# The first half of the mixer projection: two f32r terms and three products against three bf16 terms and six products

## The chip, the cores and the metric

The kernel runs on one core of a Trainium2 chip. The metric is device time in microseconds (us), from one execution of the whole program. The core has five engines that run side by side: TensorE (PE in the profile, with its weight loads listed apart as PEld), VectorE (DVE), ScalarE (ACT), GpSimd (POOL) and SyncE (SP), which here only issues DMA transfers.

## What is computed

The reference is one step of a hybrid decoder layer: a Mamba-2 part and an mLSTM part read the same projected input, their outputs are put side by side and projected back, then come cross attention to a memory and a SwiGLU block, each with norms before and after. It works on 512 prompt tokens and 8 x 8 sample tokens, 576 in all, with a model width of 1024. What matters here is one line, the mixer projection:

```
y_ssd = _rms(y_ssd.reshape(..., SSM_GROUPS, SSM_INNER // SSM_GROUPS)).reshape(...) * g_ssm_out
...
mix = jnp.concatenate([y_ssd.astype(x.dtype), h_ml.astype(x.dtype)], axis=-1) @ w_out
x = x + _rms(mix) * g_post_mix
```

All of it is float32. w_out is 2048 x 1024: its upper 1024 rows meet y_ssd, the first half, and its lower 1024 rows meet h_ml, the second half.

## The kernel before, in words

Every activation lies transposed, features on the 128 partitions, in tiles of 128 x 8 x 576 (eight k-tiles of 128 features, 576 tokens). TensorE computes one output tile of 128 features at a time; the tokens are cut into two parts of 256 and 320 columns (HALVES).

To get nearly float32 precision, both operands are split into a high term, rounded to the type float32r, and the remainder as a low term. Three products are summed in PSUM: high x high, high x low of the activation, low of the weight x high. `split_w` (line 173) does this for weights: it loads 128 x 1024 floats into a buffer "raw" (two of them) through SP's queue, casts them on ACT into whi (line 181), and subtracts on DVE into wlo (line 188); whi and wlo have three buffers each. `split` (191) does the same for activations (ACT at 192, DVE at 193). `gemm` (195) issues the three products of each k-tile (201 to 203), each a matmul with its own weight load; `gemm2` (206) takes one PSUM bank for each half of the tokens and calls an evacuation when that half is done.

The stage that the change touches runs from line 1007 to line 1138. Ahead of it stand the last tiles of the input projection (the output gate of the mLSTM, `in_tile` with `og_evac`), and between them `gn_apply` (1014) scales each k-tile of y (the tile xs of slot 5) by its gain and norm and splits it into mixs_h and mixs_l. mixs_h lies in a pool "big0" on the right side of SBUF that takes over space of the sample mLSTM's pool, closed just ahead; mixs_l lies in slot 2. The splits of the second half's activations, mixm_h and mixm_l (1031, 1032, 1038), follow in the program.

The projection's first half is the loop at line 1133: for each of eight output tiles j, `split_w` of the weights I["wout"][j, 0], then `gemm2` for the first half of the tokens in a bank of pool GP and for the second half in a bank of pool MP (three banks each), each followed by a copy on ACT into f (tile f_mix, which has slot 5, that of y). `presplit` then does a piece of work for later: it loads a weight of the attention output or of the feed-forward part, splits it on ACT and DVE, and stores its low term to memory from GpSimd. The second half of the projection, `out2` (1166), runs the same products with mixm and I["wout"][j, 1], and adds f on DVE (line 1161).

Up to here the order on each engine is the scheduler's: it simulates the program in time and lets each engine take the instruction that is ready, so instructions of neighbouring loop turns mix. `issue_after` holds an instruction back until another has been issued. Later parts of the kernel are ordered by hand.

At the very start of the kernel, line 300 runs 24 bf16 matmuls of 128 x 256 on zeros, all with the same weights, to bring TensorE to its full clock. Line 612 holds bf16 matmuls of 512 columns with 80 rows, two for each of eight feature tiles in the Mamba-2 part.

Of the kernel before, what the change touches and what calls it, by code (L numbers as in the profile page):

```python
# [11 lines left out]
F32 = mybir.dt.float32  # L12
F32R = mybir.dt.float32r
BF16 = mybir.dt.bfloat16
AF = mybir.ActivationFunctionType
ALU = mybir.AluOpType
# [3 lines left out]
P = 128  # L20
T = 576
# [3 lines left out]
KT = 8  # L25
# [3 lines left out]
HALVES = [(0, 256), (256, 320)]  # L29
# [87 lines left out]
def build(nc, tc, ctx, I, O):  # L117
    V, A, G, S, TE = nc.vector, nc.scalar, nc.gpsimd, nc.sync, nc.tensor
    mm = TE.matmul

    cp = ctx.enter_context(tc.tile_pool(name="const", bufs=1))
    wp = ctx.enter_context(tc.tile_pool(name="weights", bufs=1))
# [8 lines left out]
    def SL(slot, name, dt=F32, shape=(P, KT, T)):  # L131

        return big.tile(list(shape), dt, name=name, tag="s%d" % slot, bufs=1)
# [8 lines left out]
    def BP(name="b"):  # L142
        return pb.tile([P, 512], F32, name=name, tag="b")
# [20 lines left out]
    def PAR(k, j=None, w=1):  # L164
        a, b = _cols[k]
        return par[:, a:b] if j is None else par[:, a + j:a + j + w]
# [4 lines left out]
    loads = []  # L171

    def split_w(src, n=1024, cut=CUT, acc=False, pool=None, to=None, raw=None):
        if raw is None:
            raw = wp.tile([P, 1024], F32, name="raw", tag="raw", bufs=2)
        loads.append(S.dma_start(raw[:, :n], src))
        if to:
            split(*to, raw[:, :n])
            return to
        hi, lo = [(pool or wp).tile([P, 1024], F32R, name=k, tag=k, bufs=NWX if pool else 3) for k in ("whi", "wlo")]  # L180
        A.copy(hi[:, :n], raw[:, :n])  # L181
        for e, a, b in ((V, 0, cut), (G, cut, n)):
            if b > a and e is G and acc:

                A.activation(lo[:, a:b], hi[:, a:b].bitcast(F32), AF.Copy, scale=-1.0)  # L185
                G.dma_start(lo[:, a:b], src[:, a:b], accum_op=ALU.add)  # L186
            elif b > a:
                e.tensor_tensor(lo[:, a:b], raw[:, a:b], hi[:, a:b].bitcast(F32), op=ALU.subtract)  # L188
        return hi, lo

    def split(hi, lo, src, eng=None):
        A.copy(hi, src)
        (eng or V).tensor_tensor(lo, src, hi.bitcast(F32), op=ALU.subtract)

    def gemm(ps, units, xh, xl, t0, n, k0=0, k1=None, order=None):

        tiles = [(hi[:, j * P:(j + 1) * P], lo[:, j * P:(j + 1) * P]) for hi, lo, nk in units for j in range(nk)]
        order = order or range(len(tiles))
        for i, k in list(enumerate(order))[k0:k1]:
            (wh, wl), ah, al = tiles[k], xh(k, t0, n), xl(k, t0, n)  # L200
            mm(ps, wh, ah, start=i == 0, stop=False)  # L201
            mm(ps, wh, al, start=False, stop=False)  # L202
            m = mm(ps, wl, ah, start=False, stop=i == len(tiles) - 1)  # L203
        return m

    def gemm2(units, xh, xl, evac, name, halves=(0, 1), alloc=None, order=None, parts=HALVES):
        for i in halves:
            t0, n = parts[i]
            ps = (alloc or GP)(name)[:, :n]
            m = gemm(ps, units, xh, xl, t0, n, order=order)  # L210
            evac(t0, n, ps)
        return m

    def act(t):
        return lambda k, t0, n: t[:, k, t0:t0 + n]


    pows, ssq_mm, rops, rows = [], [], [], []
# [124 lines left out]
    stop = gemm(ps0[2][1], [(*w2, KT)], U, UL, 256, 320, 0, NSS)  # L343
# [12 lines left out]
    stop = gemm(ps0[3][0], [(*w3, KT)], U, UL, 0, 256)  # L356
# [208 lines left out]
    y = xs  # L565
# [98 lines left out]
    for g in range(2):  # L664
        ps = BP("ps_xts")
# [5 lines left out]
    ps = BP("ps_bts")  # L671
# [7 lines left out]
    for g in range(2):  # L679
        for hb in range(2):  # L680
            dst = cpad[:, g, 4 * hb:4 * hb + 4, :].rearrange("p b t -> p (b t)")
            src = bc[:, 2 + g, TP + 32 * hb:TP + 32 * hb + 32]
# [4 lines left out]
    for g in range(2):  # L687
        psb = BP("ps_ls")
        pb3 = psb.rearrange("p (h t) -> p h t", h=8)
        for h in range(8):  # L690
            mm(psb[:, h * TS:(h + 1) * TS], sel[:80, 8 * g + h:8 * g + h + 1].to_broadcast([80, P]), cumst[:, TP:T],
               start=h == 0, stop=h == 7, skip_group_check=True)
# [8 lines left out]
        for h in range(8):  # L701
            k, j = h % 2, (8 * g + h) // 2
# [6 lines left out]
    ps = BP("ps_eg")  # L709
# [6 lines left out]
    for b in range(4):  # L716
# [3 lines left out]
        for g in range(2):  # L720
            for hb in (1, 0):
# [3 lines left out]
                   start=b == 0, stop=b == 3, skip_group_check=True)  # L725
        for hb in range(2):
# [4 lines left out]
            for g in range(2):  # L731
                ps = BP("ps_hu")
# [6 lines left out]
    ps = BP("ps_yt")  # L739
# [64 lines left out]
    def head_norm(num, ex, n4, pool, name):  # L804

        ss = pool.tile([P, n4], F32, name="hn_ss", tag="hn_ss", bufs=2)
        jk = pool.tile([P, 256], F32, name="hn_jk", tag="hn_jk", bufs=1)
        for c in range(n4):
            A.activation(jk, num[:, c, 0:256], AF.Square, accum_out=ss[:, c:c + 1])
        d = pool.tile([P, n4], F32, name="hn_d", tag="hn_d", bufs=2)  # L810
        den = num[:, :, 256:257].rearrange("p c o -> p (c o)")
        V.scalar_tensor_tensor(d, den, -1.0, den, op0=ALU.mult, op1=ALU.max)
        V.tensor_tensor(d, d, ex, op=ALU.max)
        V.reciprocal(d, d)
        v = pool.tile([P, n4], F32, name="hn_v", tag="hn_v", bufs=2)
        yy = pool.tile([P, n4], F32, name="hn_y", tag="hn_y", bufs=2)
        a = pool.tile([P, n4], F32, name="hn_a", tag="hn_a", bufs=2)
        V.tensor_tensor(v, d, d, op=ALU.mult)
        V.tensor_tensor(v, v, ss, op=ALU.mult)
        V.tensor_scalar(v, v, 1.0 / 256.0, EPS, op0=ALU.mult, op1=ALU.add)  # L820
        G.tensor_tensor(yy, v, C32("nhalf")[:, :n4], op=ALU.pow)
        V.tensor_tensor(a, yy, yy, op=ALU.mult)
        V.scalar_tensor_tensor(a, a, -0.5, v, op0=ALU.mult, op1=ALU.mult)
        V.scalar_tensor_tensor(a, a, 1.5, yy, op0=ALU.add, op1=ALU.mult)
        V.tensor_tensor(a, a, d, op=ALU.mult)
        return a

    for h in range(4):
        q, k = qk[:, h, :], qk[:, 4 + h, :]
# [16 lines left out]
        for c in range(4):  # L846
# [3 lines left out]
                        op=ALU.mult)  # L850
# [16 lines left out]
        f = head_norm(num, expnm[:, :, h:h + 1].rearrange("p c o -> p (c o)"), 4, mp_, "p")  # L867
# [89 lines left out]
    for hb in range(2):  # L957
# [6 lines left out]
        for b in range(4):  # L964
# [16 lines left out]
            for h in range(4):  # L981
                ps = BP("ps_cu")
# [13 lines left out]
        f = head_norm(num, ex, 1, ms, "s")  # L996
# [9 lines left out]

    big0 = ctx.enter_context(tc.tile_pool(name="big0", bufs=1, side="right", reuse_waits="tile"))

    def SL0(name, dt=F32R):
        return big0.tile([P, KT, T], dt, name=name, tag="s0", bufs=1)  # L1010

    mixs_h = SL0("mixs_h")
    mixs_l = SL(2, "mixs_l", F32R)
    def gn_apply(g):
        rb = gn_rc[g][0][:, 0:T]
        for j in range(4 * g, 4 * g + 4):
            V.scalar_tensor_tensor(y[:, j, :], y[:, j, :], PAR("g_ssm", j), rb, op0=ALU.mult, op1=ALU.mult)
            split(mixs_h[:, j, :], mixs_l[:, j, :], y[:, j, :])


    mixm_h = SL(3, "mixm_h", F32R)
# [77 lines left out]
    f = SL(5, "f_mix")  # L1099
# [8 lines left out]
    evs, ahead = [], []  # L1108

    def presplit(n):  # L1110

        while ahead:
            n_, c, t_ = ahead.pop(0)
            h_ = at.tile([P, 1024], F32R, name="preh", tag="prh", bufs=1)
            with tc.issue_after(evs[-1].ins):
                A.copy(h_[:, c], t_[:, c])
            V.tensor_tensor(t_[:, c], t_[:, c], h_[:, c].bitcast(F32), op=ALU.subtract)
            G.dma_start(pre[:, n_, c], t_[:, c])
        for _ in range(n):
            n_ = turns.pop(0)  # L1120
            k, j = PRE[n_]
            c = slice(512 if j == 5 else 0, 1024)
            t_ = at.tile([P, 1024], F32, name="prel", tag=("pr", "prl", "mv")[n_ % 3], bufs=1)
            G.dma_start(t_[:, c], I[{"xo": "wxo", "g": "wgate", "u": "wup"}[k]][j][:, c])
            ahead.append((n_, c, t_))
# [5 lines left out]
    rmem_b = at.tile([P, 256], F32, name="rmem_b")  # L1131
    ssqm, ssq = ssq_tile("ssqm"), ssq_tile("ssqo")
    for j in range(8):
        w = split_w(I["wout"][j, 0], cut=1024)
        for i, bank in enumerate((GP, MP)):
            gemm2([(*w, KT)], act(mixs_h), act(mixs_l), lambda t0, n, ps: evs.append(A.copy(f[:, j, t0:t0 + n], ps)),
                  "ps_o1", (i,), bank)
        presplit(1 if j else 2)

        if j > 3:  # L1140
            k2 = slice(2 * j - 8, 2 * j - 6)
            with tc.issue_after(loads[-1].ins):
                S.dma_start(memraw[:, k2, :], I["memT"][:, k2, :])
# [26 lines left out]
    x = SL(1, "x1")  # L1170
# [39 lines left out]
    m = out2(7, 0)  # L1210
    with tc.issue_after(m.ins):
        rc = rstd_cols([ssq], HCHUNKS[1], "po1", alloc=B0)
    m = out2(6, 0)
# [41 lines left out]


    qh = SL0("qh")
    ql = SL(2, "ql", F32R)
    qsm = at.tile([P, 8, TS], F32, name="qsm")
# [124 lines left out]
    mk, m = mem_key(3, wm[:2])  # L1384
    with tc.issue_after(m.ins):
        rc = rstd_cols([ssq], HCHUNKS[0], "po0", alloc=B0)
    mv, m = mem_value(3, wm[2:])
# [10 lines left out]
    m = xq(4, 1)  # L1398
    with tc.issue_after(m.ins):
        rc2[1] = rstd_cols([ssq2], HCHUNKS[1], "p21", alloc=B1)  # L1400
    m = xq(5, 1)
    with tc.issue_after(m.ins):
        rstd_rows(rc2[1][:, 2:3], CHUNKS[4:], rb2, B1)
    m = xq(6, 1)
# [34 lines left out]
    f = SL(4, "f_xo")  # L1439
# [202 lines left out]
    for n_, (key, p) in enumerate(order):  # L1642
        src = I[{"xo": "wxo", "g": "wgate", "u": "wup"}[key[0]]][key[1]]
# [46 lines left out]
    class Pair:  # L1690
# [72 lines left out]
        def bank(s):  # L1763
            return (MP if s.up else GP)("ps_u" if s.up else "ps_g")[:, :288]
# [568 lines left out]
    parts = [(c, d) for c in range(2) for d in range(2)]  # L2333
    xr, xt, ft = [], {}, {}
# [156 lines left out]
```

## Time and profile before

| | |
|---|---|
| median of 3 runs | 1104.03 us (1101.62 to 1104.86) |
| the profiled execution | 1104.28 us, span 1102.5 us |
| PE matmuls, weight loads | 8351 each |
| DMA | 182.34 MB, mean 165 GB/s |

The profiled execution is one run of the program whose instructions were recorded; its span is the time from the first to the last recorded instruction. Rows of a view give line, engine, operation, the tiles written and read (out<-in) and the shapes. "x128" is a count. In a tile's view, three numbers with slashes are the least, median and greatest duration in ns, followed by the first and last start in us. In a timeline, the first two numbers are start and length in us; a row with a count merges several instructions of one form, and its length reaches from the first start to the last end. In a row of the grouped lines, the numbers behind the bar are the total busy time in us, the mean ns of one, and the idle time before them. A matmul's duration includes the time until its results have drained, so consecutive matmuls overlap, and the distance between starts is a different number.

### The profile page before, as it was taken

Reading aid. Unit: us, or ns where it says so; the run is one execution under the profiler, and the core shown is the slowest. Engines: PE = TensorE matmul, PEld = TensorE weight load, DVE = VectorE, ACT = ScalarE, POOL = GpSimd, SP = SyncE. Lnnn points to the kernel's source line nnn. Section 1 sums busy time; section 2 is a strip of 40 time slices with the busy share of each in tenths; the row PEclk is TensorE's granted clock in tenths of the full one; section 3 lists DMA queues with packets and bytes.
Section 4 is the critical chain, followed back from the end, with each engine's and each line's share of the span. In section 5 each row is a group of like instructions: output and inputs, shape, how many; then the busy total and the mean of one; then the engine's idle time right before and its main releaser. Section 6 shows DMA issues by size and latency. Waiting matters only on the chain.

```text
span 1102.5 us, 21225 instructions
## 1 busy us (share of the span) xinstructions
PE 1089.3 (99%) x8351; PEld 1042.0 (95%) x8351; DVE 771.4 (70%) x1521; ACT 604.0 (55%) x1121; POOL 215.3 (20%) x301
## 2 busy tenths in 40 slices
PE   9999999999999999999999999999999999999997
PEld 8999889898998999999988889999999999999997
DVE  6797765558786784578755556676578879888655
ACT  6768523246563465566535445634565556555654
POOL 1333442323122121110144401100000210020000
PEclk9999999999999999999999999999999999999999
DMA  6776553425474438773477755652552863497432
GB/s 205 178 148 154 121 160 126 155 83 158 130 202 108 127 99 287 284 278 100 154 272 268 287 168 169 208 184 66 179 152 82 203 161 89 102 230 211 108 133 86
DMA packets 59432, 182.34 MB, mean 165 GB/s; under 512 B 6556, under 2 KB 10780, under 8 KB 58820
## 3 DMA queue, kind: packets, MB, share of 16 engines
q1 hardware_dynamic: 44324, 142.19, 38.4%
q0 software_dynamic: 14720, 38.28, 16.6%
q8 instruction: 65, 1.06, 0.4%
q10 hardware_dynamic: 288, 0.52, 0.1%
q14 instruction: 35, 0.29, 0.1%
HBM read 151.66 MB, written 29.30 MB: 164 GB/s over the span
## 4 chain that ended last, share of the span: by engine, by line
PE 82%; DVE 5%; DMA 4%; ACT 3%; issue 1%; POOL 0%; DVEq 0%; ACTq 0%; SPq 0%
PE ps_in L201 5%; PE ps_in L202 5%; PE ps_in L203 5%; PE ps_g L1770 3%; PE ps_g L1771 3%; PE ps_g L1772 3%; PE ps_u L1770 3%; PE ps_u L1771 3%; PE ps_u L1772 3%; PE ps_o L201 2%; PE ps_o L203 2%; PE ps_o L202 2%; PE ps_dn L201 2%; PE ps_dn L203 2%; PE ps_dn L202 2%; PE ps_dn L1978 2%
## 5 line engine op out<-in xcount | busy, mean ns | idle before, releaser
L203 PE MATMUL ps_in<-uh,wlo 128*128 128x256 f32 (+1 forms) x544 | 163.8, 301 | 0.7 <-DMA wlo<-win 0.4
L202 PE MATMUL ps_in<-ul,whi 128*128 128x256 f32 (+1 forms) x544 | 163.9, 301 | 0.0
L201 PE MATMUL ps_in<-uh,whi 128*128 128x256 f32 (+1 forms) x544 | 163.7, 301 | 0.0
L181 ACT CAST whi<-raw 128x1024 fp32r<-128x1024 f32 (+1 forms) x102 | 102.7, 1011 | 83.5 <-PE ps_in L202 28.7
L188 DVE TENSOR_TENSOR wlo<-raw,whi 128x512 fp32r<-128x512 f32 (+1 forms) x94 | 91.2, 972 | 50.6 <-ACT whi L181 48.8
L202 PEld LDWEIGHTS ps_in<-ul,whi 128*128 128x128 f32 x544 | 103.0, 189 | 2.9 <-issue 2.2
L203 PEld LDWEIGHTS ps_in<-uh,wlo 128*128 128x128 f32 x544 | 103.0, 190 | 2.4 <-DVE wlo L188 0.6
L201 PEld LDWEIGHTS ps_in<-uh,whi 128*128 128x128 f32 x544 | 103.0, 189 | 2.0 <-issue 0.8
L186 POOL DMA_DIRECT2D wlo<-win x32 | 28.0, 883 | 80.8 <-ACT wlo L185 64.2
L1770 PE MATMUL ps_g<-b,whi 128*128 128x288 f32 x144 | 42.5, 296 | 0.2 <-ACT cc L1829 0.2
L1771 PE MATMUL ps_u<-b,whi 128*128 128x288 f32 x144 | 42.5, 295 | 0.0
L1771 PE MATMUL ps_g<-b,whi 128*128 128x288 f32 x144 | 42.5, 295 | 0.0
L1770 PE MATMUL ps_u<-b,whi 128*128 128x288 f32 x144 | 42.5, 295 | 0.0
L201 PE MATMUL ps_xo<-qh,whi 128*128 128x288 f32 x128 | 38.3, 302 | 0.4 <-ACT whi L181 0.3
L203 PE MATMUL ps_o<-mixm_h,wlo 128*128 128x256 f32 (+1 forms) x128 | 38.1, 298 | 0.0
L201 PE MATMUL ps_o<-mixm_h,whi 128*128 128x256 f32 (+1 forms) x128 | 38.0, 297 | 0.0
L202 PE MATMUL ps_o<-mixm_l,whi 128*128 128x256 f32 (+1 forms) x128 | 37.9, 296 | 0.0
L203 PE MATMUL ps_xq<-u2h,wlo 128*128 128x320 f32 (+1 forms) x128 | 37.9, 296 | 0.0
L202 PE MATMUL ps_xq<-u2l,whi 128*128 128x320 f32 (+1 forms) x128 | 37.8, 297 | 0.0
L201 PE MATMUL ps_xq<-u2h,whi 128*128 128x320 f32 (+1 forms) x128 | 37.8, 300 | 0.0
L202 PE MATMUL ps_xo<-ql,whi 128*128 128x288 f32 x128 | 37.7, 295 | 0.0
L203 PE MATMUL ps_xo<-qh,wlo 128*128 128x288 f32 x128 | 37.5, 295 | 0.0
(785 smaller groups left out, 3895.3 us busy)
## 6 DMA issues: line engine op xcount, KB each, us to landing
raw<-win SPq DMA_DIRECT2D x35, 512.0 KB, 3.6
raw<-wout SPq DMA_DIRECT2D x17, 512.0 KB, 5.6
raw<-wxq SPq DMA_DIRECT2D x13, 512.0 KB, 3.7
raw<-wgate SPq DMA_DIRECT2D x13, 512.0 KB, 4.4
raw<-wup SPq DMA_DIRECT2D x13, 512.0 KB, 4.0
wlo<-win POOLq DMA_DIRECT2D x24, 256.0 KB, 5.6
kva<-kc SPq DMA_DIRECT2D x12, 512.0 KB, 6.5
kva<-vc SPq DMA_DIRECT2D x12, 512.0 KB, 6.6
```

The source lines that it names most:

```text
L181: A.copy(hi[:, :n], raw[:, :n])
L186: G.dma_start(lo[:, a:b], src[:, a:b], accum_op=ALU.add)
L188: e.tensor_tensor(lo[:, a:b], raw[:, a:b], hi[:, a:b].bitcast(F32), op=ALU.subtract)
L201: mm(ps, wh, ah, start=i == 0, stop=False)
L202: mm(ps, wh, al, start=False, stop=False)
L203: m = mm(ps, wl, ah, start=False, stop=i == len(tiles) - 1)
L1770: mm(ps, wh, b[0][:, k, :], start=start and k == 0, stop=False, skip_group_check=True)
L1771: mm(ps, wh, b[1][:, k, :], start=False, stop=False, skip_group_check=True)
L1772: m = mm(ps, wl, b[0][:, k, :], start=False, stop=k == 3, skip_group_check=True)
L1978: mm(ps, wh, bh, start=start and k == 0, stop=False, skip_group_check=True)
```

## The change

The first half of the projection gets three bf16 terms for each operand. `split3` makes them: a cast of x to bf16 (h), x minus h in place, a cast of the rest (m), and the rest minus m as the third term (l): two casts on ACT and two subtractions on DVE, in a chain, and x is overwritten. `split3_w` loads a weight tile as before and splits it; h and m share a buffer of the ring whi, l takes one of wlo. `gemm3` walks k, then the three weight terms, then the two halves of the tokens, then the activation terms: three with the first weight term, two with the second, one with the third. That makes six products per k-tile and half. Both banks are evacuated when the whole tile is done. mixs is now a tile of 16 x 576 bf16 for h and m in the place of mixs_h, and one for l in slot 2. The second half of the projection stays as it was.

```diff
+    def split3(dst, x):
+        h, m, l = dst
+        A.copy(h, x)
+        V.tensor_tensor(x, x, h, op=ALU.subtract)
+        A.copy(m, x)
+        V.tensor_tensor(l, x, m, op=ALU.subtract)
+
+    def split3_w(src):
+        raw = wp.tile([P, 1024], F32, name="raw", tag="raw", bufs=2)
+        loads.append(S.dma_start(raw, src))
+        a, b = [wp.tile([P, 2048], BF16, name=k, tag=k, bufs=3) for k in ("whi", "wlo")]
+        w = a[:, 0:1024], a[:, 1024:2048], b[:, 0:1024]
+        split3(w, raw)
+        return w
+
+    def gemm3(banks, w, x3, parts):
+        for k in range(KT):
+            for i, wt in enumerate(w):
+                for ps, (t0, n) in zip(banks, parts):
+                    for xt in x3[:3 - i]:
+                        mm(ps, wt[:, k * P:(k + 1) * P], xt[:, k, t0:t0 + n], start=k == 0 and i == 0 and xt is x3[0],
+                           stop=k == KT - 1 and i == 2)
...
-    mixs_h = SL0("mixs_h")
-    mixs_l = SL(2, "mixs_l", F32R)
+    mixs = SL0("mixs_hm", BF16, 2 * KT)
+    mixs = mixs[:, 0:KT, :], mixs[:, KT:2 * KT, :], SL(2, "mixs_l", BF16, (P, 2 * KT, T))[:, 0:KT, :]
...
-            split(mixs_h[:, j, :], mixs_l[:, j, :], y[:, j, :])
+            split3([t_[:, j, :] for t_ in mixs], y[:, j, :])
...
-        w = split_w(I["wout"][j, 0], cut=1024)
-        for i, bank in enumerate((GP, MP)):
-            gemm2([(*w, KT)], act(mixs_h), act(mixs_l), lambda t0, n, ps: evs.append(A.copy(f[:, j, t0:t0 + n], ps)),
-                  "ps_o1", (i,), bank)
+        w = split3_w(I["wout"][j, 0])
+        banks = [bank("ps_o1")[:, :n] for bank, (_, n) in zip((GP, MP), HALVES)]
+        gemm3(banks, w, mixs, HALVES)
+        for ps, p in zip(banks, HALVES):
+            evs.append(A.copy(f[:, j, p[0]:p[0] + p[1]], ps))
```

More of the change, by code (lines that the diff above doesn't have):

```diff
@@ L1007, in build, with SL0 @@
     big0 = ctx.enter_context(tc.tile_pool(name="big0", bufs=1, side="right", reuse_waits="tile"))
-    def SL0(name, dt=F32R):
-        return big0.tile([P, KT, T], dt, name=name, tag="s0", bufs=1)
-    mixs_h = SL0("mixs_h")
-    mixs_l = SL(2, "mixs_l", F32R)
+    def SL0(name, dt=F32R, kt=KT):
+        return big0.tile([P, kt, T], dt, name=name, tag="s0", bufs=1)
+    mixs = SL0("mixs_hm", BF16, 2 * KT)
+    mixs = mixs[:, 0:KT, :], mixs[:, KT:2 * KT, :], SL(2, "mixs_l", BF16, (P, 2 * KT, T))[:, 0:KT, :]
     def gn_apply(g):
```

## The prediction

> **What bounds the kernel now.** First the page, for which engine is never free:
>
> ```profile
> span 1102.5 us, 21225 instructions
> PE 1089.3 (99%) x8351; PEld 1042.0 (95%) x8351; DVE 771.4 (70%) x1521; ACT 604.0 (55%) x1121; POOL 215.3 (20%) x301
> PEclk9999999999999999999999999999999999999999
> ```
>
> TensorE (PE) is busy for 99% of the span at the full granted clock; VectorE (DVE) and ScalarE (ACT) have 30% and 45% free. So time is gained or lost by the matmul stream, unless a stage proves otherwise. The stage in question is eight output tiles with 48 matmuls each, 384 in all. The tile view of ps_o places it:
>
> ```profile
> L201 PE MATMUL ps_o<-mixs_h,whi x128: 279/298/317, 396.8 to 447.4; 128*128 128x256 f32 x64, 128*128 128x320 f32 x64
> L203 PE MATMUL ps_o<-mixs_h,wlo x128: 279/294/315, 397.6 to 447.7; 128*128 128x256 f32 x64, 128*128 128x320 f32 x64
> L201 PE MATMUL ps_o<-mixm_h,whi x128: 278/296/395, 447.9 to 502.1; 128*128 128x320 f32 x64, 128*128 128x256 f32 x64
> ```
>
> The windows are, from the start of the first mixs matmul to the start of the first mixm one, for the tile ps_o alone, and then for all work in this stage and in those around it:
>
> ```profile
> 396.82:447.87 51.05, 51.05 (x385) 50.99 (x385) 0.00 (x0) 5.75 (x15) 1.00 0.66 234
> 380.00:396.50 16.50, 16.50 (x123) 16.23 (x122) 11.09 (x40) 6.35 (x14) 3.33 (x4) 1.00 0.30 104
> 396.70:448.00 51.30, 51.30 (x387) 51.24 (x387) 33.23 (x44) 32.42 (x56) 8.98 (x15) 1.00 0.66 234
> 447.70:505.00 57.30, 56.08 (x424) 55.51 (x423) 38.79 (x70) 35.33 (x59) 8.16 (x15) 1.00 0.74 257
> ```
>
> The columns are window, length, then busy time and count of PE, weight loads (PEld), DVE, ACT, POOL (the first row has no POOL), granted clock, DMA share and GB/s. PE has no free time in this stage: 51.05 us for 384 matmuls is 132.9 ns each (x385 counts one that only begins at the edge). DVE is free for 18 us of it, ACT for 19. So the stage's length is the number of matmuls times the distance from one start to the next. That distance, not the duration in the rows, is the price, because matmuls overlap:
>
> ```profile
> 398.10 0.31 PE L201 MATMUL ps_o<-mixs_h,whi 128*128 128x320 f32 x1
> 398.24 0.28 PE L202 MATMUL ps_o<-mixs_l,whi 128*128 128x256 f32 x1
> 398.36 0.28 PE L203 MATMUL ps_o<-mixs_h,wlo 128*128 128x256 f32 x1
> 398.48 0.28 PE L201 MATMUL ps_o<-mixs_h,whi 128*128 128x256 f32 x1
> ```
>
> Starts are 140 ns apart after 320 columns and 120 ns after 256, while each matmul "lasts" about 300 ns. The distance follows the columns that stream through, and both have the same 128-column weights.
>
> **The matmuls.** The change takes away 8 tiles x 8 k x 2 halves x 3 products = 384 matmuls and puts in 8 x 8 x 2 x 6 = 768, of the same sizes (128x256 and 128x320, mean 288 columns), in bf16. Half the bytes help only if a bf16 column takes less time. The trace of before has few bf16 matmuls. The nearest are the 24 at the start, 128x256 with 128x128 weights, repeated on the same weights, a load for each; the last five of them ran at the full clock:
>
> ```profile
> 4.98 0.71 PE L300 MATMUL ps_warm<-wz 128*128 128x256 bf16 x5
> L300 PEld LDWEIGHTS <-wz x24: 98/152/152, 1.1 to 5.3; 128*128 128x128 bf16 x24
> L300 PE MATMUL ps_warm<-wz x24: 272/421/421, 1.1 to 5.4; 128*128 128x256 bf16 x24
> 248.00 0.61 PE L612 MATMUL ps_l<-cumst,c 80*128 80x512 bf16 x2
> L612 PE MATMUL ps_l<-cumst,c x16: 377/381/392, 134.0 to 248.2; 80*128 80x512 bf16 x16
> ```
>
> Five in 0.71 us, the last one lasting 0.272 (the minimum, at the full clock), start (0.71 - 0.272) / 4 = 109.5 ns apart: 0.428 ns per column, so 123.2 ns for 288. That is 7% below the 132.9 of now, nowhere near half. The other bf16 row is a pair in the middle of the kernel, 512 columns: 0.61 - 0.381 = 0.23 us apart, 0.447 ns per column, so 129 ns for 288. And if bf16 went no faster than f32r, 132.9 stays. The new stage is then:
>
> - by the first row 768 x 123.2 ns = 94.6 us, which is 43.6 more than 51.05;
> - by the pair 768 x 129 = 99.1 us, 48.0 more;
> - at today's distance 768 x 132.9 = 102.1 us, 51.0 more.
>
> I take the first: same rows, same weights, same columns, and five in a stream, where the pair stands alone with 80 rows. The other two stay as the upper end.
>
> "Both halves in a row" puts up to six matmuls on one weight term. A gain would need that a load is left out or that loads set the pace. Neither shows: the page has 8351 loads for 8351 matmuls, and the 24 of L300, which do repeat one weight tile, have 24 loads. So I put the order at nothing.
>
> A rule that would make it worth more is weighed here. The loads get shorter: 98 ns in the row above, against 188 for the f32 ones:
>
> ```profile
> L203 PEld LDWEIGHTS ps_o<-mixs_h,wlo 128*128 128x128 f32 x128 | 24.1, 189 | 0.0
> L202 PEld LDWEIGHTS ps_o<-mixs_l,whi 128*128 128x128 f32 x128 | 24.0, 188 | 0.1
> ```
>
> The Trainium skill ("TensorE: Matmul & The Clock Gate", section "Weight-path perf modes — Fast Weight Load (FWL) and DoubleRow") says that full 128-column weights that are not fp32 load faster, measured about 2x. The two rows agree with it (98 against 188). The same place says that it wins with few columns per matmul; were the loads the pace here, halving the distance to 66.5 ns would make 768 matmuls cost 51 us and the change nothing. What the distances say of that stands with the rivals.
>
> **The weight splits.** A split now is one cast and one subtraction of 128x1024; it becomes two of each, in a chain of four over the same raw tile, written over in place:
>
> ```profile
> L188 DVE TENSOR_TENSOR wlo<-raw,whi 128x1024 fp32r<-128x1024 f32 x8 | 9.8, 1219 | 0.9 <-ACT whi L181 0.9
> L181 ACT CAST whi<-raw 128x1024 fp32r<-128x1024 f32 x8 | 8.4, 1046 | 1.1 <-PE ps_o L202 1.1
> ```
>
> Eight tiles add 8 x 1.05 = 8.4 us to ACT and 8 x 1.22 = 9.8 to DVE. The chain of one tile becomes 2 x (1.05 + 1.22) = 4.5 us, and one tile of matmuls will last 94.6 / 8 = 11.8, so it is hidden; only the first two fall in the stage before, where DVE has 16.5 - 11.1 = 5.4 us free per 16.5 and ACT 10. If that cover failed, the first tile would come 1.05 + 1.22 = 2.3 us late. The raw tile is held that much longer, so the next weight load, queued on SP for that buffer, goes out 2.3 us later; there are two raw buffers and a tile every 11.8 us. The slots are the same three of 4 KB a partition (hi and mid share one). Priced at nothing.
>
> **The activation splits.** These are at the edge, because the first matmuls wait for them; the casts begin at 395.8, a microsecond ahead of PE:
>
> ```profile
> 395.82 4.69 ACT L192 CAST mixs_h<-xs 128x576 fp32r<-128x576 f32 x8
> 396.53 0.76 DVE L193 TENSOR_TENSOR mixs_l<-xs,mixs_h 128x576 fp32r<-128x576 f32 x1
> 397.61 4.76 DVE L193 TENSOR_TENSOR mixs_l<-xs,mixs_h 128x576 fp32r<-128x576 f32 x7
> 396.82 0.55 PE L201 MATMUL ps_o<-mixs_h,whi 128*128 128x256 f32 x3
> ```
>
> Eight casts take 4.69 us on ACT, seven subtractions 4.76 on DVE (0.68 each); both double. DVE then needs 16 x 0.68 = 10.9 us from 396.5, to about 407.9 with the 0.4 of other work it does between. PE consumes the eight k-tiles of its first output tile in 11.8 us, to 408.6. So production keeps just ahead if casts and subtractions of neighbouring k-tiles overlap, and I add 1 us for the start, where mid needs cast, subtraction and cast (0.67 + 0.76 + 0.67 = 2.1 us) before it exists, against the 12 x 0.123 = 1.5 us that PE has per k-tile. If each k-tile's chain of four ran alone, 2.9 us each, eight take 22.9 us and PE would wait about 11. Behind these, queued on DVE and ACT, are the splits of the other half's activations (mixm), first used a whole stage later, and the evacuation into f_mix, which takes the buffer of y and so waits for its last subtraction, about 408; a tile has three banks in each pool, so PE doesn't feel it.
>
> **The rest.** 16 evacuations stay; both of a tile now come at its end, and the next tile has other banks. The 1.2 us that PE is idle in the next stage (57.30 - 56.08) may shrink, since DVE, ACT and the DMA queues get 44 us more to run ahead; I count that only in the low end.
>
> **Sum.** +43.6 (matmuls) + 1.0 (start) = +44.6 us on the profiled execution of 1104.28 us (span 1102.5): 1148.9. The median of the runs shown, 1104.03, lies 0.25 below it: 1148.6.
>
> **Rivals.** *Same pace as f32r*: the 9 ns gained in L300 come from repeating one tile on an idle memory, and in the stage, with DMA at 0.66, bf16 takes 132.9. For it: the pair at L612 at 129. Then +51.0 + 1.0, so 1156.0.
>
> *The splits starve the first tile*: the chain of four runs k-tile by k-tile. Then 11 us of waiting instead of 1, about 1159. Against it: now ACT runs its eight casts without waiting for the subtractions.
>
> *No slower, because loads set the pace.* PEld is busy 50.99 of 51.05 us, as full as PE. If a matmul cannot start sooner because its weights take 188 ns, bf16's 98 ns brings the distance to 132.9 x 98 / 188 = 69.3 ns: 768 x 69.3 = 53.2 us, +2.2, and 1106.2. It decides at (51.05 + 3.3) / 768 = 71 ns; below that the change costs less than the 0.3%, 3.3 us, that a measurement of this kernel can tell from none. The Trainium skill ("Perfetto Trace Analysis", section "Identifying the Most-Contended Engine") indeed says to judge TensorE by matmul FLOPs and by the busy share of LDWEIGHTS rather than by matmul busy time; taken so, 95% would name the loads. Against it in the rows: with equal loads the distance goes with the columns (120 and 140 ns), and L300, with loads of 98 ns, still starts only every 109.5.
>
> *It doesn't do what it says*: the scheduler, which orders instructions itself, breaks up the rows of equal weights. By the above that costs nothing.
>
> **How the numbers follow.** Forecast 0.81, same pace 0.11, starving 0.05, loads 0.02 (no slower), 0.01 for a gain I don't see. Predicted 1148.6. The low end is the forecast without the start and with the 1.2 us regained, and 1% off the stage for the rounding of 0.71: 1148.6 - 1.0 - 1.2 - 1.0 = 1145.4, so 1145. The high end takes in the pair and the same pace, 1157. Slower by over 0.3%: 0.97; within: 0.02; faster: 0.01.
>
> **What would show it.** PE count 8735 (+384), PEld too. In the stage, starts 109 to 110 ns apart after 256 columns and about 137 after 320; first matmul still near 397, second half beginning near 492, everything behind it shifted by 44 to 45 us and otherwise alike. Sixteen casts and sixteen subtractions of 128x576 from 395.8 to about 408, with PE idle for around 1 us before its second tile. I am wrong if the stage's 768 matmuls start 71 ns apart or less, if fewer than 8735 loads appear and the stage is shorter than 94 us, or if PE's idle time in the first tile is over 3 us.

## The result and the profile after

The changed kernel takes 1163.24 us (median of 4 runs, 1162.78 to 1164.86) against 1102.82 us for the kernel before in the same comparison: a ratio of 1.0538, with a 95% interval of 1.0513 to 1.0564. That is about 60 us slower. The forecast was 44.6 us slower, and 1163 lies above the top of its range, 1157. The profiled execution took 1162.78 us, its span is 1161.0, 58.5 more than before.

The page of the changed kernel, the lines that answer to those shown of before:

```profile
span 1161.0 us, 22029 instructions
PE 1135.6 (98%) x8735; PEld 1067.3 (92%) x8735; DVE 786.5 (68%) x1537; ACT 616.3 (53%) x1137; POOL 216.8 (19%) x301
PEclk9999999999999889999999999999999999999999
```

PE has 384 more matmuls and as many more loads, as forecast: no load is left out. But its busy share is lower, and the clock row, all nines before, has two eights where the new stage begins. The window view of ps_o, from the first mixs matmul to the first mixm one (columns as before):

```profile
401.94:507.89 105.95, 97.21 (x769) 0.03 (x1) 0.00 (x0) 4.85 (x14) 0.93 0.43 142
```

(This view does not count the bf16 loads with the tile, hence the 0.03; over all tiles they take 76.22 us in this window.) The same view of all work, in the stretch at the low clock and behind the stage, reads:

```profile
399.90:417.00 17.10, 6.33 (x26) 3.63 (x26) 16.97 (x27) 15.16 (x27) 4.13 (x6) 0.50 0.34 124
507.89:1161.00 653.11, 644.60 (x4976) 626.81 (x4973) 454.85 (x853) 359.18 (x681) 89.76 (x95) 1.00 0.56 168
```

The stage has grown from 51.05 to 105.95 us, begins at 401.9 in place of 396.8, and PE works in 97.2 of it. For 17.1 us the granted clock is 0.50, and in that stretch PE is busy for 6.3 us while DVE and ACT are full (17.0 and 15.2). What follows the stage takes 653.11 us; in the kernel before, by the same view:

```profile
447.87:1102.50 654.63, 644.55 (x4975) 626.47 (x4973) 456.05 (x854) 359.53 (x681) 92.11 (x100) 1.00 0.56 172
```

So the 58.5 us lie in the stage and at its start. What PE waited for, by the view of waits:

```profile
PE ps_o L240 <- ACT mixs_hm L222: 6.4, 1, 6.4
PE ps_o L240 <- ACT mixs_hm L220: 4.3, 1, 4.3
PE ps_o L240 <- DVE mixs_l L223: 2.3, 1, 2.3
```

The columns are total, times, longest. Each wait is for one term of the activations: 4.3 us for the first high term (L220), 6.4 for the first mid term (L222), 2.3 for the first low one (L223), 13.0 in all. The timelines show why they come late. PE, with the wait before each first matmul in brackets:

```profile
397.23 0.38 PE L1027 MATMUL ps_hts<-c,hns 128*128 128x128 f32 x2
401.94 1.60 PE L240 MATMUL ps_o<-mixs_hm,whi 128*128 128x256 bf16 x6 [4.33 <-ACT mixs_hm L220]
409.97 1.60 PE L240 MATMUL ps_o<-mixs_hm,whi 128*128 128x256 bf16 x6 [6.43 <-ACT mixs_hm L222]
413.87 0.64 PE L240 MATMUL ps_o<-mixs_l,whi 128*128 128x256 bf16 x2 [2.30 <-DVE mixs_l L223]
```

ACT, which casts:

```profile
397.55 1.06 ACT L220 CAST whi<-raw 128x1024 bf16<-128x1024 f32 x1
398.50 2.56 ACT L1057 ACTIVATE mixm_h<-qk,ghalf 128x512 fp32r<-128x512 f32 x4
401.21 4.69 ACT L220 CAST mixs_hm<-xs 128x576 bf16<-128x576 f32 x8
406.48 1.94 ACT L1057 ACTIVATE mixm_h<-qk,ghalf 128x512 fp32r<-128x512 f32 x3
408.31 1.04 ACT L222 CAST whi<-raw 128x1024 bf16<-128x1024 f32 x1
409.25 4.68 ACT L222 CAST mixs_hm<-xs 128x576 bf16<-128x576 f32 x8
```

DVE, which subtracts:

```profile
399.78 2.73 DVE L1058 SCALAR_TENSOR_TENSOR mixm_l<-qk,ghalf,mixm_h 128x512 fp32r<-128x512 f32 x4
402.77 5.43 DVE L221 TENSOR_TENSOR xs<-xs,mixs_hm 128x576 f32<-128x576 f32 x8
413.07 5.43 DVE L223 TENSOR_TENSOR mixs_l<-xs,mixs_hm 128x576 bf16<-128x576 f32 x8
```

The scheduler did not let the chains of neighbouring k-tiles overlap. It put all eight high casts, then all eight subtractions, then all eight mid casts, then all eight low subtractions; and ahead of and between these phases it put work that is due later: the splits of the second half's activations (mixm, L1057 and L1058) and of the third output tile's weights (whi, at 397.55 and 408.31). So the first mid term exists at 409.9 and the first low one at 413.8, when PE had been free since 397.6. PE meanwhile does six products of high terms, one in each of its six banks (three output tiles, two halves), and stops.

The distances, on the other hand, are those of the sum. From the PE timeline later in the stage:

```profile
420.61 0.27 PE L240 MATMUL ps_o<-mixs_l,whi 128*128 128x256 bf16 x1
420.72 0.43 PE L240 MATMUL ps_o<-mixs_hm,whi 128*128 128x320 bf16 x2
420.99 0.30 PE L240 MATMUL ps_o<-mixs_l,whi 128*128 128x320 bf16 x1
421.13 0.65 PE L240 MATMUL ps_o<-mixs_hm,whi 128*128 128x256 bf16 x4
```

0.11 us after 256 columns and 0.14 after 320 (0.27 for two).

### The profile page after: what moved, and what is told of

Its sections match the earlier page's. It is cut to its first block, busy times and chain, and to the rows that moved or that the text cites. A ratio compares the mean times of both kernels' runs of the same rounds, so it can differ in the third digit from the quotient of the medians.

```text
span 1161.0 us, 22029 instructions
## 1 busy us (share of the span) xinstructions
PE 1135.6 (98%) x8735; PEld 1067.3 (92%) x8735; DVE 786.5 (68%) x1537; ACT 616.3 (53%) x1137; POOL 216.8 (19%) x301
## 4 chain that ended last, share of the span: by engine, by line
PE 84%; DVE 4%; DMA 4%; ACT 3%; issue 1%; POOL 1%; DVEq 0%; ACTq 0%; SPq 0%; POOLq 0%
PE ps_o L240 8%; PE ps_in L201 4%; PE ps_in L202 4%; PE ps_in L203 4%; PE ps_g L1797 3%; PE ps_g L1798 3%; PE ps_g L1799 3%; PE ps_u L1797 3%; PE ps_u L1798 3%; PE ps_u L1799 3%; PE ps_dn L201 2%; PE ps_dn L203 2%; PE ps_dn L202 2%; PE ps_dn L2005 2%; PE ps_dn L2006 2%; PE ps_v L808 2%
## 5 line engine op out<-in xcount | busy, mean ns | idle before, releaser
L181 ACT CAST whi<-raw 128x1024 fp32r<-128x1024 f32 (+1 forms) x94 | 94.4, 1008 | 111.7 <-PE ps_o L240 26.6
L188 DVE TENSOR_TENSOR wlo<-raw,whi 128x512 fp32r<-128x512 f32 (+1 forms) x86 | 81.3, 947 | 77.5 <-ACT whi L181 75.9
L240 PE MATMUL ps_o<-mixs_hm,whi 128*128 128x320 bf16 (+1 forms) x512 | 90.9, 292 | 10.8 <-ACT mixs_hm L222 6.4
L240 PEld LDWEIGHTS <-whi 128*128 128x128 bf16 x640 | 63.7, 99 | 29.2 <-issue 13.9
L240 PE MATMUL ps_o<-mixs_l,whi 128*128 128x256 bf16 (+1 forms) x128 | 36.3, 289 | 2.3 <-DVE mixs_l L223 2.3
```

What stands on the lines that cost most here:

```text
L240: mm(ps, wt[:, k * P:(k + 1) * P], xt[:, k, t0:t0 + n], start=k == 0 and i == 0 and xt is x3[0], stop=k == KT - 1 and i == 2)
```

## The experiments

The theory after the result: the 768 matmuls cost what was forecast, and the 16 us beyond it are the three waits and the halved clock around them. The rivals: the stage is long through the bf16 matmuls themselves, or the equal weights in a row matter after all. All ratios are against the kernel before, run on the same chip; the changed kernel's is 1.0538 (1.0513 to 1.0564).

**The chain first.** The chains of the k-tiles are interleaved by force, and everything that stood between is held behind them.

```diff
+            with tc.issue_after(chain[j - 2][0].ins) if j > 1 else ExitStack(), \
+                    tc.issue_after(chain[j - 2][1].ins) if j > 1 else ExitStack():
+                chain.append(split3([t_[:, j, :] for t_ in mixs], y[:, j, :]))   # returns the m cast and the l subtraction
...
+    with tc.issue_after(chain[7][0].ins), tc.issue_after(chain[7][1].ins):
         for j in range(8):      # the mixm splits; also split3_w for j > 1
```

> The changed kernel, with the activation splits forced into the order h0 h1 m0 h2 m1 ... on ScalarE and s0 s1 l0 s2 l1 ... on VectorE, and with the splits of the second half's activations and of the third and later weight tiles held behind them. Nothing is left out. Theory A (the 768 matmuls cost what was forecast, 94 us; the other 16 us are TensorE waiting 13.1 us for mid and low terms, and its halved clock after it): the first casts move from 401.2 to about 398, TensorE waits 2 to 4 us in the first tile in place of 13.1, the clock stays up or drops shortly, time 1148 to 1153 us. Rival B (the stage is long because of the bf16 matmuls themselves): no change, 1161 to 1165 us.

1150.14 us, ratio 1.0422 (1.0397 to 1.0446). Its waits for the terms:

```profile
PE ps_o L239 <- ACT mixs_hm L222: 1.2, 1, 1.2
PE ps_o L239 <- ACT mixs_hm L220: 1.1, 1, 1.1
PE ps_o L239 <- DVE mixs_l L222: 0.4, 1, 0.4
```

Its stage in the window view of ps_o:

```profile
397.69:495.05 97.36, 95.82 (x768) 0.03 (x1) 0.00 (x0) 4.92 (x14) 0.98 0.44 150
```

The waits fall from 13.0 to 2.7 us, the stage from 105.95 to 97.36, and the whole kernel by 13 us, with all 768 matmuls still there. The rival that the bf16 matmuls are slow is out; 1150.1 is 1.5 us above the forecast of 1148.6.

**The other work later, the phases left.** Only the second of the two edits.

> The changed kernel, with only the second half's activation splits and the third and later weight splits held behind the last mid cast and the last low subtraction; the four phases (eight h, eight subtractions, eight m, eight l) are left as the scheduler puts them. Nothing is left out. Theory A: the phases start at about 398 without other work between them, m0 follows h7 at about 402.5 and l0 at about 404, so TensorE waits 5 to 7 us, with some of the clock drop left: 1154 to 1158 us. Rival A2 (the phase order does the harm, not the other work ahead of it): still about 10 us of waiting, 1159 to 1164 us.

1154.97 us, ratio 1.0467 (1.0442 to 1.0492). The mid term is now late by its phase alone, as the timeline of ACT shows:

```profile
397.67 4.68 ACT L220 CAST mixs_hm<-xs 128x576 bf16<-128x576 f32 x8
402.94 4.67 ACT L222 CAST mixs_hm<-xs 128x576 bf16<-128x576 f32 x8
```

Its waits:

```profile
PE ps_o L239 <- ACT mixs_hm L222: 4.6, 1, 4.6
PE ps_o L239 <- ACT mixs_hm L220: 1.1, 1, 1.1
PE ps_o L239 <- DVE mixs_l L222: 0.4, 1, 0.4
```

Waits of 6.1 us, as expected.

**The interleaving alone.** Only the first of the two edits.

> The changed kernel with only the forced order h0 h1 m0 h2 m1 ... and s0 s1 l0 s2 ...; the second half's activation splits and the third weight tile stay where the scheduler puts them, between. Nothing is left out. If both things do harm on their own (phases 5 us, other work ahead 8 us, from the two runs before), this gives 1156 to 1161 us. If the interleaving alone suffices: 1148 to 1152 us. If it is worth nothing without the other: 1161 to 1165 us or above.

1157.13 us, ratio 1.0469 (1.0424 to 1.0513), waits of 4.3, 3.0 and 0.9 us. So each of the two edits saves about as much: 8 us and 6 us alone (0.7% by either ratio), and 13 us (1.2%) together.

**The high and mid terms earlier.** No order is forced; two tiles change places.

```diff
-    mixs = SL0("mixs_hm", BF16, 2 * KT)
-    mixs = mixs[:, 0:KT, :], mixs[:, KT:2 * KT, :], SL(2, "mixs_l", BF16, (P, 2 * KT, T))[:, 0:KT, :]
+    mixs = SL(2, "mixs_hm", BF16, (P, 2 * KT, T))
+    mixs = mixs[:, 0:KT, :], mixs[:, KT:2 * KT, :], SL0("mixs_l", BF16, 2 * KT)[:, 0:KT, :]
```

> The changed kernel with one placement changed: the tile of the high and mid terms lies in slot 2, which is free earlier, and the low terms in the place of mixs_h. Nothing is left out and no order is forced. Casts, first subtractions and mid casts can then run under the output gate's matmuls, and only the eight low subtractions (5.4 us) are left at the edge. Theory A (TensorE's waits are the chain left without cover): its waits at the edge fall from 13.1 to 0 to 2 us, the clock stays up, 1146 to 1150 us, as forecast before. Rival (work moved ahead delays the output gate's evacuations instead): 1152 us or above.

1149.87 us, ratio 1.0401 (1.0357 to 1.0445). The timeline of ACT:

```profile
380.59 4.69 ACT L220 CAST mixs_hm<-xs 128x576 bf16<-128x576 f32 x8 [1.92 <-PE ps_c L885]
```

and that of PE:

```profile
399.17 0.41 PE L240 MATMUL ps_o<-mixs_l,whi 128*128 128x256 bf16 x2 [2.60 <-DVE mixs_l L223]
```

The high casts run at 380.6, under the matmuls of the stage before, against 397.7 in the kernel that only moves the other work: their place comes free 17 us sooner. PE waits once, 2.6 us (a little over the 0 to 2 expected), for the low terms; the 1.1 us for the first high term, which remain with the chain first, are gone. The buffer, which the prediction took as given, was the lever.

**f32r with the chain of four.** The kernel before, with only the activation split made as long as the new one (the last subtraction's result is not used).

```diff
-            split(mixs_h[:, j, :], mixs_l[:, j, :], y[:, j, :])
+            A.copy(mixs_h[:, j, :], y[:, j, :])
+            V.tensor_tensor(y[:, j, :], y[:, j, :], mixs_h[:, j, :].bitcast(F32), op=ALU.subtract)
+            A.copy(mixs_l[:, j, :], y[:, j, :])
+            V.tensor_tensor(y[:, j, :], y[:, j, :], mixs_l[:, j, :].bitcast(F32), op=ALU.subtract)
```

> The kernel before, f32r and three products, with only the activation splits of the first half turned into the chain of four (cast, subtraction in place, cast of the rest into the low term, one more subtraction whose result nobody reads). Nothing is left out. Theory A (the chain, not bf16, makes TensorE wait): the low term of the first k-tile exists only behind all eight casts and the mixm casts that the scheduler puts between, near 405 in place of 397.3, so TensorE waits 4 to 8 us, and its clock drops: 1107 to 1114 us. Rival (the waiting belongs to the bf16 kernel's weights or order): 1101 to 1105 us.

1112.71 us, ratio 1.0076 (1.0047 to 1.0105). Its waits in the stage:

```profile
PE ps_o L201 <- ACT whi L181: 4.0, 1, 4.0
PE ps_o L202 <- ACT mixs_l L1020: 3.4, 1, 3.4
```

The stage in the window view of ps_o:

```profile
396.65:457.93 61.28, 53.89 (x385) 53.31 (x386) 0.00 (x0) 5.91 (x15) 0.92 0.65 224
```

The first wait is put down to the weights of the third output tile. PE comes to them so early because the first two tiles stand still without their low term: after four products of high terms it stops, where in the kernel before the first product with the low term follows at 397.35. Without any bf16, PE waits 7.4 us in the same place, and its 384 matmuls take 53.9 us in place of 51.05 at a mean clock of 0.92. The chain alone makes the stall.

**Two bf16 terms.** The third terms and their three products are left out in this and the next two kernels.

```diff
-        V.tensor_tensor(x, x, h, op=ALU.subtract)
-        A.copy(m, x)
-        V.tensor_tensor(l, x, m, op=ALU.subtract)
+        V.tensor_tensor(m, x, h, op=ALU.subtract)
...
-            for i, wt in enumerate(w):
+            for i, wt in enumerate(w[:2]):
...
-                    for xt in x3[:3 - i]:
+                    for xt in x3[:2 - i]:
```

> The changed kernel with two bf16 terms and three products (the third term of weights and activations and the three products with the smallest weight are left out, so that the result is less exact). Theory A, by the distance of 109 and 136 ns: 384 x 122.5 ns = 47.0 us for the stage in place of 51.05 before, so 1098 to 1100 us, with no starvation, since the chain is again one cast and one subtraction. Rival B (bf16 goes at 132.9 or slower in the stage): 1102 to 1104 us or above.

1107.2 us, ratio 1.0027 (1.0013 to 1.0042): the stage came out as expected, the time did not. The window view of ps_o:

```profile
396.39:443.35 46.96, 46.96 (x385) 0.03 (x1) 0.00 (x0) 4.80 (x14) 1.00 0.63 218
```

of all work, from there to the query projection's first matmul:

```profile
443.35:515.42 72.07, 67.27 (x502) 66.79 (x500) 49.19 (x92) 43.51 (x78) 8.70 (x16) 0.95 0.68 238
```

and the longest wait in that stretch:

```profile
PE ps_ss L250 <- DVE ssqm L291: 4.8, 1, 4.8
```

384 matmuls in 46.96 us are 122.3 ns each (123.2 forecast), 4.1 us less than in f32r. But the stretch behind it takes 72.07 us; in the kernel before it is 66.35:

```profile
447.87:514.22 66.35, 65.13 (x501) 64.56 (x500) 48.01 (x91) 42.20 (x76) 8.16 (x15) 1.00 0.67 233
```

PE reaches the memory norm's sums earlier, waits 4.8 us there (1.2 before) and loses clock behind that (0.95). The gain is given back, and more: from there to the end it takes 590.78 us in place of 588.28, with a wait of 2.4 us for the sums of a later norm (0.5 before).

**The memory norm later.** The same kernel, with one call moved.

```diff
-    memory_norm()
     for j in range(4, 8):
         out2(j, 1)
+    memory_norm()
```

> Two bf16 terms and three products (the third term and its products are left out, as in the run with two terms), and the memory norm's sums, for which TensorE waited 4.8 us there, moved behind the next four half tiles of the second half. Theory: the 4.1 us gained in the stage are no longer given back to that wait and the halved clock behind it: 1097 to 1101 us. Rival (the wait only moves on to another point, since ScalarE, VectorE and the transfers of the second half set its pace): 1104 to 1108 us.

1103.6 us, ratio 1.0000 (0.9981 to 1.0018). That wait is gone, but PE now waits elsewhere, by the view of waits:

```profile
PE ps_os L1370 <- DMA kva<-vc: 2.0, 2, 1.1
PE ps_o L203 <- DVE wlo L188: 1.6, 2, 0.9
PE ps_o L201 <- ACT whi L181: 1.1, 1, 1.1
```

2.7 us for weight splits in the second half and 2.0 for a transfer in the attention (0.4 before). The time lies between what the theory gave (at most 1101) and the rival (at least 1104), nearer to the rival: the 4.1 us are gone by the end, and these waits, behind the stage, are the ones that are new.

**Both halves in two terms.** The kernel just above, with the second half in bf16 too.

```diff
-    mixm_h = SL(3, "mixm_h", F32R)
-    mixm_l = SL(4, "mixm_l", F32R)
+    mixm_h = SL(3, "mixm_h", BF16, (P, 2 * KT, T))[:, 0:KT, :]
+    mixm_l = SL(4, "mixm_l", BF16, (P, 2 * KT, T))[:, 0:KT, :]
...
+            kept2[j] = split3_w(I["wout"][j, 1])[:2]
```

> As the run before it, with the second half of the projection in two bf16 terms and three products too (third terms left out in both halves). By the distances 384 x 10.4 ns = another 4 us off: 1093 to 1097 us. Rival (the second half is already paced by the splits and transfers around it): no better than the run with one half, 1097 to 1104 us.

1103.47 us, ratio 0.9998 (0.9983 to 1.0012), as the rival said, with waits of 3.1 us for subtractions and 2.2 for casts of the second half's weights. The gain in matmul time does not reach the end. No version found beats the kernel before.

**The order of the products.** First without equal weights in a row: half by half, in the order hh, mh, hm, lh, mm, hl (weight term first). By the program's order, only one of twelve neighbouring pairs has equal weights (the one between the two halves of a k-tile); in the changed kernel nine do.

```diff
-            for i, wt in enumerate(w):
-                for ps, (t0, n) in zip(banks, parts):
-                    for xt in x3[:3 - i]:
+            for ps, (t0, n) in zip(banks, parts):
+                for m, (i, q) in enumerate(((0, 0), (1, 0), (0, 1), (2, 0), (1, 1), (0, 2))):
```

> The changed kernel with the six products of a k-tile in another order: half by half, and no two neighbouring matmuls with the same weight term. Nothing is left out. If equal weights in a row are worth nothing: 1161 to 1166 us and the same distances of 109 and 136 ns. If they save part of the loads: the distances grow and the time goes to 1170 us or above.

1158.3 us, ratio 1.0499 (1.0473 to 1.0525): neither expectation. Its waits in the stage:

```profile
PE ps_o L239 <- ACT whi L222: 4.9, 1, 4.9
PE ps_o L239 <- ACT mixs_hm L220: 4.3, 1, 4.3
```

At the full clock, from 430 to 500 us in the window view of ps_o, the changed kernel and then this one:

```profile
430.00:500.00 70.00, 70.00 (x574) 0.00 (x0) 0.00 (x0) 4.15 (x12) 1.00 0.48 156
430.00:500.00 70.00, 70.00 (x575) 0.00 (x0) 0.00 (x0) 4.66 (x12) 1.00 0.48 166
```

574 matmuls in 70 us against 575: equal weights in a row are worth nothing. The waits, however, are 9.2 us in place of 13.0. The second is put down to the mid cast of the third weight tile, which ACT does at 408.3, right ahead of the mid casts of the activations (409.26): PE meets the weight term first, and both come late together. That suggested that within a bank the products run in the order of the program, so that the order decides how many can run before a late term is needed. The next kernel orders them by activation term.

```diff
-            for i, wt in enumerate(w):
-                for ps, (t0, n) in zip(banks, parts):
-                    for xt in x3[:3 - i]:
+            for q, xt in enumerate(x3):
+                for i, wt in enumerate(w[:3 - q]):
+                    for ps, (t0, n) in zip(banks, parts):
```

> The changed kernel with the products of a k-tile ordered by activation term: the three with h, the two with m, the one with l. Nothing is left out; the chain of splits stays as it is. If a bank's products run in program order, TensorE in the changed kernel can do only one product in each of its six banks before it needs a mid term; here it can do three, 18 in all, inside the wait for m0. Expected: the second wait falls from 6.4 to 3 to 5 us and the third from 2.3 to about 1, 1157 to 1161 us. Rival (the order within a bank doesn't matter): 1161 to 1165 us.

1161.1 us, ratio 1.0501 (1.0449 to 1.0554). Its waits in the stage:

```profile
PE ps_o L240 <- ACT mixs_hm L220: 4.3, 1, 4.3
PE ps_o L240 <- ACT whi L222: 3.9, 1, 3.9
PE ps_o L240 <- DVE wlo L223: 1.2, 1, 1.2
```

They are 9.4 us in all, the second and third about as long as expected. PE now does 14 products before the second wait, where it did six in the changed kernel, so the order within a bank does matter; it is not 18, because the mid term of the third weight tile comes late too. The waiting went down by 3.6 us; the time, at the upper edge of what was expected, does not differ clearly from the changed kernel's.

**The clock.** Matmuls on constants, whose results are not used, are put ahead of the first k-tile's products with the high, the mid and the low term.

```diff
+    dummy = [B1("dummy")]      # MP("dummy") in the second of the two kernels
...
+                idle(38)       # so many 128x256 matmuls of an identity on a constant
+                for i in range(3):
+                    one(k, i, 0, True)
+                idle(55)
+                for i in range(2):
+                    one(k, i, 1, True)
+                idle(20)
+                one(k, 0, 2, True)
```

> The changed kernel with 38, 55 and 20 bf16 matmuls of 128x256 on constants, into a bank that nobody reads, put where TensorE waited 4.3, 6.4 and 2.3 us for the high, mid and low terms; the first k-tile's products are ordered by activation term for that. Nothing is left out. If the halved clock from 399.9 to 417.0 us comes from those waits, the clock stays at full there and the time falls by 2 to 4 us to 1159 to 1161 us, with the waits themselves still there. If the clock has another cause: 1162 to 1165 us.

1166.2 us, ratio 1.0562 (1.0530 to 1.0593). A failed try: the first 38 of them themselves had to wait for a bank, began at 401.26 after a wait of 3.76 us, and pushed the real work back.

With a free bank:

> The filler run again, with the 38, 55 and 20 matmuls on constants in a bank that is free at once; in the first try they themselves waited 3.8 us for a bank and so came late. Nothing is left out. If the halved clock comes from TensorE's waits: full clock through the edge and 2 to 4 us less than the changed kernel, 1159 to 1161 us; the waits for the terms remain. If the clock has another cause: halved as before, 1162 us or above.

1163.56 us, ratio 1.0520 (1.0473 to 1.0566): no clear gain in the whole time. But the window of all work in its stage and behind it reads

```profile
402.54:504.70 102.16, 102.16 (x844) 82.41 (x843) 42.73 (x54) 38.60 (x63) 11.74 (x20) 1.00 0.43 147
504.70:1162.00 657.30, 646.23 (x4976) 628.42 (x4973) 454.24 (x853) 359.03 (x681) 89.53 (x95) 1.00 0.55 167
```

In the stage the clock is 1.00 throughout. The order by activation term is not the reason: in the kernel above that has this order and no filling, the clock is 0.50 from 400.6 to 417.5. So the halved clock does come from the waits, and the stage ends at 504.7, 3.2 us before the changed kernel's 507.9. The rest then takes 657.3 us against 653.1, so those 3.2 us are lost again behind it. PE is idle there for 11.1 us (657.30 - 646.23) in place of 8.5; 1.5 us of it go to the sums of a later norm and 2.0 to two transfers of the attention (0.3 for such a transfer in the changed kernel). Why these come late is open.

## Why the prediction was wrong

The sum of the 58.5 us, from the rows above: matmuls, 768 x 122.3 ns = 93.9, less 51.05, +42.9; waits +13.0; matmuls at the halved clock, 97.2 - 93.9, +3.3; the stage before ends at 397.6 in place of 396.8, +0.8; everything behind the stage 653.1 in place of 654.6, -1.5.

- **The matmul term** (+43.6) held: 122.3 ns each in the stage with no wait (two bf16 terms, 384 in 46.96 us), and the same in the changed kernel from 417.0 us on (743 in 90.89 us), +42.9 for 768; with the chain first, where 2.7 us of waits are left, the 768 take 95.8 us in place of the 94.6 forecast. Taking the price from the warm-up row, and not from the pair of 512 columns, was right.
- **The order of the weights at nothing** held for the loads, but not altogether: through the order within a bank it changes the waiting by nearly 4 us (13.0 against 9.2 and 9.4).
- **The weight splits priced at nothing** did not hold: the third tile's two casts (1.06 and 1.04 us) stood on ACT ahead of and between the activation splits, and in the two other orders it is this tile's mid term that PE waits for (4.9 and 3.9 us).
- **The step that failed is "production keeps just ahead if casts and subtractions of neighbouring k-tiles overlap, and I add 1 us for the start".** The waits were 13.0 us and the clock took 3.3 more: 16.3 in place of 1. The condition did not hold. The prediction's own sign of being wrong, over 3 us of idle time in the first tile, came (6.4 and 2.3 us). The prediction named a starving first tile as a rival, at 11 us and 0.05, with another mechanism (k-tile by k-tile); what came was phase by phase. That this rival's time, about 1159, lies nearer to 1163 than the forecast is luck. The evidence against that rival, that the eight casts run without waiting for the subtractions, does speak against k-tile by k-tile. But it fits the order by phases, which the prediction did not weigh: the scheduler that ran eight independent casts in a row ran them ahead of the dependent ones here too.
- **"Behind these, queued on DVE and ACT"** was wrong as well: most of the mixm splits stood ahead of and between the phases. In the kernel before they do stand behind the eight casts, and the prediction kept that order; the scheduler ordered the changed kernel anew. From the timeline of ACT before:

```profile
401.36 4.40 ACT L1031 ACTIVATE mixm_h<-qk,ghalf 128x512 fp32r<-128x512 f32 x7
```

- **The clock was left out.** A stall of PE was priced at its own length, without the 3.3 us that the matmuls lost to the halved clock around it.
- **The loads rival** fell: with loads half as long (98 ns, from 82.41 us for 843 in the stage with the filling matmuls, against 188), the distance fell by 8%, not by half. The Trainium skill ("Perfetto Trace Analysis", section "Identifying the Most-Contended Engine") says to judge how near to its limit TensorE is by matmul FLOPs and by the busy share of the weight loads. Here that share misleads: in the stage before, the loads were busy for 50.99 of 51.05 us and did not bind, and in the changed kernel from 417.0 us on they are busy for only 72.60 of 90.89 us, with the matmuls just as dense.

## What to carry to other kernels

When a change makes the chain ahead of a busy engine longer, price it from when the first of its results can exist, in the order that the scheduler gives, and ask which buffer lets it start earlier: giving a tile a place that comes free 17 us sooner was worth as much as forcing the whole order. A stall of TensorE here cost its length and the slow clock around it (13.0 and 3.3 us). And a stage made faster gains only until the next wait for something that runs at its own pace: the 4 us gained by two terms were gone before the next 72 us were over.

## What the runs showed of the hardware

The halved clock comes in steps. The stretches at a granted clock of 0.50 are 17.1 us long in the changed kernel, and 6.8 us (478.80 to 485.60) at the 4.8 us wait of the first two-term kernel, by the window view:

```profile
478.80:485.60 6.80, 4.55 (x18) 4.58 (x19) 5.73 (x11) 4.74 (x9) 1.05 (x3) 0.50 0.91 305
```

Both are multiples of 3.4 us (five and two). The Trainium skill ("TensorE: Matmul & The Clock Gate", section "What's actually happening") gives a free-running window of 3.4 us in which activity is judged, and half rate as the state after an idle one. The lengths agree with that. That a whole window must be idle first does not: in the kernel with the high and mid terms early, the only wait near is one of 2.6 us (396.57 to 399.17), and the clock is at 0.50 behind it for one step, from 399.7 to 403.1:

```profile
399.80:403.10 3.30, 3.30 (x14) 1.98 (x13) 3.30 (x6) 1.30 (x2) 0.00 (x0) 0.50 0.40 149
```

The measurement decides here: a wait shorter than a step was enough.
